# Two attention layers: scores of each head from its own 64 rows, rotation read from PSUM

## The chip, the core and the metric

The kernel runs on one core of a Trainium2 chip. What counts is the time of one execution on the device, in microseconds (us). TensorE (PE in the profile) multiplies matrices and writes its results to PSUM, which has eight banks per partition; VectorE (DVE), ScalarE (ACT) and GpSimd (POOL) work between PSUM and SBUF; SyncE (SP) starts transfers. Each engine goes through its own list of instructions in order and waits at semaphores for the others.

## What is computed

The program holds two blocks of a model on one sequence of 256 tokens, with 16 meta tokens in front (T = 272 columns). The first block has four layers: attention (layer 0), an mLSTM, an HGRN2, attention again (layer 3). The change is in the two attention layers, which compute this:

```
q, k, v, z = split(u @ w_in)                   # 16 query heads, 4 key heads, 64 features each
q = rope(rmsnorm(q, q_gain), pos)              # per head; rope: x1*cos - x2*sin, x2*cos + x1*sin
k = rope(rmsnorm(k, k_gain), pos)              # x1, x2 = first and second 32 features
s = q . k / 8                                  # a block of 128 queries: its own 128 keys and those before
s = where(0 <= dist < 128 and valid, s, -inf)
m = max(max(s), sink)
p = exp(s - m) / (sum(exp(s - m)) + exp(sink - m))
y = (p @ v) * silu(z) @ w_out
```

## The kernel before

**Layout.** Features lie on partitions and tokens on columns. A tile of 128 features holds two heads. The layer works in two halves `hf`, each with one key tile, four query tiles `n` and one value tile: 2 key heads and 8 query heads. Before, the columns of the weights were permuted (`turned`), so that a tile's 128 rows are: first 32 features of head 0, first 32 of head 1, second 32 of head 0, second 32 of head 1. So the rotation swaps the upper and the lower 64 rows, but the rows of one head are not together. To separate the two heads, `key` writes two copies of K (`kp`), each with the other head's rows set to zero.

**Projections.** A projection tile is 24 matmuls (8 groups of weight rows, each as three passes L402, L403, L404 of split high and low parts); half a tile, 12 matmuls, is the `unit` in which the order of TensorE is counted. The split weights `whi` and `wlo` come by two ways: a DMA by SP with a cast L389 on ScalarE and a subtraction L395 on VectorE, or DMAs by POOL (L329, L337) with a pass L336 on ScalarE between them.

**Key and query.** `key` and `query` take a finished projection from PSUM: Square for the norm (L695, L742), a copy with the gain (L697, L745), two copies of 64 rows for the swapped halves (`swap`, L594), then on VectorE a product with cos, a product with sin and a sum (L699 to L701, L751 to L753). A matmul over the squares gives the sums for the norm (L705, L759).

**Scores.** One step of `scores` (L831 to L856) takes one query block `bq` (1 or 2) and one tile n: a matmul L838 of 128 rows against both masked K copies, 2 x 144 or 2 x 256 columns in one bank, and a matmul L839 that adds the mask; then the maximum (L843, VectorE), small operations (L844 to L846), one exp for the sink (L847), one exp per head with its sum (L850, ScalarE), and the division (L852 to L855). `turn` (L863 to L868) transposes p on TensorE, `values` (L878, L880) multiplies by v, `gate` (L922) and a split (L585, L586) make the input `MH`, `ML` of the output projection, which runs in two parts of 96 matmuls, the second one for the features of the second half. Layer 0 has also a first block of 16 queries, done by `short`.

**Order.** TensorE's order is written by hand: `Flow` keeps a list of due times in units, and after each half tile it puts in what is due. Steps follow each other `D_ST` units apart (A0_ST = 1.5, A3_ST = 1), eight in a half; `turn` comes `D_PT` units after its step. The other engines' orders are made by a scheduler. PSUM banks by name (`PB`): mm 3, s 2, t 1, g 1, a 1; scores take from s, projections from mm.

## Time and profile before

| | before |
|---|---|
| three runs | 1418.65, 1420.56, 1421.35 us |
| median | 1420.56 us |
| profiled execution | 1422.77 us |
| its span (first to last instruction) | 1421.0 us |
| mean granted TensorE clock | 0.993 |
| TensorE busy | 1356.4 us, 95% |
| VectorE / ScalarE / POOL busy | 992.2 / 804.6 / 446.6 us |

Start times in all rows count from the start of the span. Layer 0 lies between some 15 and 128 us, layer 3 between some 637 and 742 us. "Busy" is the sum of an engine's instructions; matmuls overlap in their pipeline, so the distance from one start to the next tells more than a matmul's own duration. In brackets stands the idle time of an engine before an instruction and who ended it.

### The profile page before, as it was taken

To read this page: it belongs to the slowest core of one execution; us is meant where nothing else is said; L and a number is where in the kernel's file an instruction comes from. 1 tells how busy PE (TensorE), PEld (TensorE's weight loads), DVE (VectorE), ACT (ScalarE), POOL (GpSimd) and SP (SyncE) were. 2 spreads that over 40 slices of the span, in tenths; PEclk is the share of its full clock that TensorE was granted. 3 is DMA by queue.
4 is the path that set the end of the run, shared out by engine and by line. 5 is a ranking of instruction groups with operands and counts; after the bars stand their busy time and mean duration, and the time that the engine had idled before them with its cause. 6 is when DMAs were issued, how large, how long until landed. Compare 5 with 4: busy or idle time off the path is not lost.

```text
span 1421.0 us, 27398 instructions
## 1 busy us (share of the span) xinstructions
PE 1356.4 (95%) x10347; PEld 1261.1 (89%) x10347; DVE 992.2 (70%) x2424; ACT 804.6 (57%) x1700; POOL 446.6 (31%) x611
## 2 busy tenths in 40 slices
PE   6999999999899999998999999999999899999997
PEld 5878989999899888898778888999999789899986
DVE  5865569999776767687656676787645576687744
ACT  6875655556644454448675586454444667455532
POOL 3322468778703434123224511300014340400000
PEclk9999999999999999999999999999999999999999
DMA  9989999999568988559889973456564994466662
GB/s 275 283 186 209 230 242 247 231 238 242 135 185 234 253 180 196 134 179 247 191 171 237 259 193 104 144 189 195 180 198 151 265 239 125 119 193 194 186 184 89
DMA packets 79349, 281.88 MB, mean 198 GB/s; under 512 B 9024, under 2 KB 10184, under 8 KB 79216
## 3 DMA queue, kind: packets, MB, share of 16 engines
q0 software_dynamic: 44512, 160.74, 49.0%
q1 hardware_dynamic: 34272, 118.60, 26.0%
q8 instruction: 81, 1.33, 0.4%
q10 hardware_dynamic: 432, 0.79, 0.1%
q14 instruction: 52, 0.43, 0.1%
HBM read 279.01 MB, written 1.07 MB: 197 GB/s over the span
## 4 chain that ended last, share of the span: by engine, by line
PE 72%; DVE 10%; DMA 6%; ACT 5%; issue 4%; POOL 2%; SPq 0%; DVEq 0%; POOLq 0%; ACTq 0%
PE pmm L402 14%; PE pmm L403 14%; PE pmm L404 14%; DMA wraw<-in_wts_dram 2%; PE ps L404 2%; PE ps L403 2%; PE ps L402 2%; DVE wlo L395 2%; DMA wlo<-in_wts_dram 2%; PE ps L838 1%; DMA whi<-in_wts_dram 1%; PE pa L878 1%; PE ps L1270 1%; PE pt L863 1%; PE pmm L1893 1%
## 5 line engine op out<-in xcount | busy, mean ns | idle before, releaser
L402 PE MATMUL pmm<-XH,whi 128*128 128x272 f32 (+1 forms) x1544 | 458.1, 298 | 17.5 <-ACT whi L389 10.8
L404 PE MATMUL pmm<-XH,wlo 128*128 128x272 f32 (+1 forms) x1544 | 444.8, 289 | 8.5 <-DMA wlo<-in_wts_dram 7.9
L403 PE MATMUL pmm<-XL,whi 128*128 128x272 f32 (+1 forms) x1544 | 445.4, 289 | 2.6 <-DVE XL L533 2.6
L389 ACT CAST whi<-wraw 128x1024 fp32r<-128x1024 f32 (+1 forms) x211 | 217.8, 1033 | 242.5 <-DMA wraw<-in_wts_dram 180.4
L395 DVE TENSOR_TENSOR wlo<-wraw,whi 128x1024 fp32r<-128x1024 f32 (+1 forms) x211 | 256.5, 1217 | 96.5 <-PE pmm L404 43.3
L402 PEld LDWEIGHTS pmm<-XH,whi 128*128 128x128 f32 x1544 | 294.4, 191 | 31.7 <-ACT whi L389 10.8
L404 PEld LDWEIGHTS pmm<-XH,wlo 128*128 128x128 f32 x1544 | 294.9, 191 | 10.0 <-DMA wlo<-in_wts_dram 8.5
L403 PEld LDWEIGHTS pmm<-XL,whi 128*128 128x128 f32 x1544 | 295.0, 191 | 4.4 <-DVE XL L533 3.7
L336 ACT ACTIVATE wlo<-whi 128x1024 fp32r<-128x1024 f32 (+1 forms) x150 | 157.9, 1054 | 86.4 <-PE pmm L404 39.8
L337 POOL DMA_DIRECT2D wlo<-in_wts_dram x150 | 130.5, 873 | 212.3 <-ACT wlo L336 101.1
L402 PE MATMUL pmm<-MH,whi 128*128 128x256 f32 (+1 forms) x624 | 182.3, 292 | 0.6 <-DVE HT L966 0.6
L329 POOL DMA_DIRECT2D whi<-in_wts_dram x150 | 89.5, 598 | 296.7 <-PE pmm L404 235.9
L403 PE MATMUL pmm<-ML,whi 128*128 128x256 f32 (+1 forms) x624 | 177.9, 285 | 1.5 <-DVE ML L586 0.8
L404 PE MATMUL pmm<-MH,wlo 128*128 128x256 f32 (+1 forms) x624 | 177.3, 284 | 0.0
L402 PEld LDWEIGHTS pmm<-MH,whi 128*128 128x128 f32 x624 | 117.7, 189 | 7.8 <-issue 6.2
L403 PEld LDWEIGHTS pmm<-ML,whi 128*128 128x128 f32 x624 | 117.9, 189 | 2.2 <-DVE ML L586 1.1
L404 PEld LDWEIGHTS pmm<-MH,wlo 128*128 128x128 f32 x624 | 118.1, 189 | 0.0
L404 PE MATMUL ps<-XH,wlo 128*128 128x256 f32 (+1 forms) x256 | 72.5, 284 | 1.4 <-DVE wlo L395 1.4
L403 PE MATMUL ps<-XL,whi 128*128 128x256 f32 (+1 forms) x256 | 72.9, 285 | 0.0
L402 PE MATMUL ps<-XH,whi 128*128 128x256 f32 (+1 forms) x256 | 72.0, 283 | 0.0
L404 PEld LDWEIGHTS ps<-XH,wlo 128*128 128x128 f32 x256 | 48.7, 190 | 1.6 <-DVE wlo L395 1.6
L403 PEld LDWEIGHTS ps<-XL,whi 128*128 128x128 f32 x256 | 48.4, 189 | 0.0
(933 smaller groups left out, 2870.2 us busy)
## 6 DMA issues: line engine op xcount, KB each, us to landing
wraw<-in_wts_dram SPq DMA_DIRECT2D x209, 512.0 KB, 4.4
whi<-in_wts_dram POOLq DMA_DIRECT2D x148, 512.0 KB, 6.4
wlo<-in_wts_dram POOLq DMA_DIRECT2D x148, 512.0 KB, 7.8
wraw<-in_wts_dram SPq DMA_DIRECT2D x16, 384.0 KB, 3.5
nb<-drb POOLq DMA_DIRECT2D x8, 272.0 KB, 6.4
HT<-in_xt_dram SPq DMA_DIRECT2D x4, 272.0 KB, 9.7
nb<-drf POOLq DMA_DIRECT2D x8, 128.0 KB, 4.9
whi<-in_wts_dram POOLq DMA_DIRECT2D x2, 384.0 KB, 6.9
```

The lines of the kernel that those rows point to most:

```text
L329: nc.gpsimd.dma_start(hi[:, :c1 - c0], src)
L336: act(lo[:, :w], hi[:, :w].bitcast(F32), AF.Copy, scale=-1.0)
L337: nc.gpsimd.dma_start(lo[:, :w], src, accum_op=ALU.add)
L389: nc.scalar.copy(hi[:, :c1 - c0], raw[:, :c1 - c0])
L395: V.tensor_tensor(lo[:, :c1 - c0], raw[:, :c1 - c0], hi[:, :c1 - c0].bitcast(F32), op=ALU.subtract)
L402: PE.matmul(ps, c.hi(b), xh, start=first, stop=False)
L403: PE.matmul(ps, c.hi(b), xl, start=False, stop=False)
L404: PE.matmul(ps, c.lo(b), xh, start=False, stop=last)
L838: PE.matmul(sv, qp[:, n, qs], kp[:, :, k0:k1], start=True, stop=False)
L863: PE.transpose(pt[:c1 - c0, (2 * y + x) * P:(2 * y + x + 1) * P], p_[:, x, c0:c1], K["ident"])
L878: PE.matmul(po[64 * x:64 * x + 64, :], vt[:kk, bq - 1 + y, 64 * x:64 * x + 64], pT[:kk, y, x].rearrange("p n t -> p (n t)"), start=y == 0, ...
L1270: PE.matmul(sl[:, 0:P], s["kw"], halves_of(kq, CB_[0], T + CA[0], b), start=True, stop=True)
```

## The change

- The weights' columns are no longer permuted: a head's 64 features lie together, head 0 in rows 0 to 63 and head 1 in rows 64 to 127.
- `scores(n)` now does both query blocks of a tile n at once. Each head has a bank of its own: four matmuls with 64 rows each (two blocks, two heads), then one mask matmul of 400 columns per bank. So a step takes both s banks; a half has four steps, A0_ST = 3 and A3_ST = 2.5 units apart. The exps of the sinks go in one instruction of four columns.
- The masked copies of K are gone; only for `short` in layer 0 two copies of 16 columns (`k0`) remain.
- `rotate` reads the projection from PSUM: four copies of 32 rows on ScalarE, a product from PSUM on VectorE, a product, a sum. The gains are in four tables (`kc`, `ks`, `qc`, `qs`), made once in each of the two layers on POOL from cos and sin and two columns of gains.
- p_ has four buffers instead of three.

The core of the diff:

```diff
-A0_KN, A0_VT, A0_QN, A0_RS, A0_AT, A0_ST, A0_PT, A0_VA, A0_S0, A0_START = 2, 2, 2, 5, 1, 1.5, 4.5, 1, 6.5, 8
-A3_KN, A3_VT, A3_QN, A3_RS, A3_AT, A3_ST, A3_PT, A3_VA, A3_S0, A3_START = 1.5, 2, 3, 5.5, 2.5, 1, 4, 1, 6, 10.5
+A0_KN, A0_VT, A0_QN, A0_RS, A0_AT, A0_ST, A0_PT, A0_VA, A0_S0, A0_START = 2, 2, 2, 5, 1, 3, 4.5, 1, 6.5, 8
+A3_KN, A3_VT, A3_QN, A3_RS, A3_AT, A3_ST, A3_PT, A3_VA, A3_S0, A3_START = 1.5, 2, 3, 5.5, 2.5, 2.5, 4, 1, 6, 10.5
...
-    head = p // 32 % 2
+    head = p // 64
     put("blk", (head[:, None] == head[None]).astype(np.float32))
-    put("selH", (head[:, None] == np.arange(2)[None]).astype(np.float32))
+    put("selA", (head[:, None] == np.arange(2)[None]).astype(np.float32))
+    put("selH", ((p // 32 % 2)[:, None] == np.arange(2)[None]).astype(np.float32))
...
-    sg = np.where(p < 64, -1.0, 1.0).astype(np.float32)[:, None]
+    sg = np.where(p % 64 < 32, -1.0, 1.0).astype(np.float32)[:, None]
...
+        if "A2" in names:
+            K["A12"] = t.bitcast(BF)[:, CB.at["A1"] - o:CB.at["A2"] - o + CB.size["A2"]]
...
+    HEADS = ((0, 32, 32), (32, 0, 32)) + LATENT
...
+            def table(n):
+
+                if n not in tables:
+                    first_consts()
+                    tables[n] = [wk.tile([P, T], F32, name=n + x, bufs=1) for x in "cs"]
+                    for t, x, g in zip(tables[n], ("cosA", "sinA"), (f"a{n}g", f"a{n}s")):
+                        G.tensor_scalar(t, K[x], smc(g, j), None, op0=ALU.mult)
+                return tables[n]
+
+            tables = {}
+
+            def rotate(ps, n, c0, dst):
+
+                c, si = (t[:, c0:] for t in table(n))
+                sw = wk.tile([P, T], F32, name="sw", bufs=SWB)[:, c0:]
+                for d, s_, m in HEADS:
+                    nc.scalar.copy(sw[d:d + m], ps[s_:s_ + m])
+                V.tensor_mul(dst, ps, c)
+                V.tensor_mul(sw, sw, si)
+                V.tensor_add(dst, dst, sw)
...
-                    act(kg, psk, AF.Copy, scale=smc("akg", j))
-                    ks = swap(wk, kg, HALVES)
-                    V.tensor_mul(kg, kg, K["cosA"])
-                    V.tensor_mul(ks, ks, K["sinA"])
-                    V.tensor_add(kg, kg, ks)
+                    rotate(psk, "k", 0, kg)
...
-                        V.tensor_mul(kg, kg, rk)
-                        kp = wk.tile([P, 2, T], F32, name="kp")
-                        for x in range(2):
-                            act(kp[:, x], kg, AF.Copy, scale=K["selH"][:, x:x + 1])
-                        D["kp"] = kp
+                        D["kp"] = wk.tile([P, T], F32, name="kp")
+                        V.tensor_mul(D["kp"], kg, rk)
+                        if not last:
+                            D["k0"] = wk.tile([P, 2, NM], F32, name="k0")
+                            for x in range(2):
+                                act(D["k0"][:, x], D["kp"][:, :NM], AF.Copy, scale=K["selA"][:, x:x + 1])
...
-                    qg = wk.tile([P, T], F32, name="qg", bufs=3)
-                    act(qg[:, q0:], psq, AF.Copy, scale=smc("aqg", j))
                     if n == 0:
                         D["qp"] = wk.tile([P, 4, T], F32, name="qp")
-                    qp = D["qp"]
-
-                    qs = swap(wk, qg, HALVES, q0)
-                    V.tensor_mul(qp[:, n, q0:], qg[:, q0:], K["cosA"][:, q0:])
-                    V.tensor_mul(qs[:, q0:], qs[:, q0:], K["sinA"][:, q0:])
-                    V.tensor_add(qp[:, n, q0:], qp[:, n, q0:], qs[:, q0:])
+                    rotate(psq, "q", q0, D["qp"][:, n, q0:])
...
-                        PE.matmul(ps0[:NM, 32 * n:32 * n + 32], qp[:, n, 0:NM], kp[:, :, 0:NM], start=True, stop=True)
+                        PE.matmul(ps0[:NM, 32 * n:32 * n + 32], qp[:, n, 0:NM], D["k0"], start=True, stop=True)
...
-                def scores(bq, n, pT):
-                    qs = slice(*BLOCKS[bq])
-                    k0, k1 = (0, 144) if bq == 1 else (16, 272)
-                    nk = k1 - k0
-                    mk = K["A1"] if bq == 1 else K["A2"]
-                    ps = mx("s")
-                    sv = ps[:, :2 * nk].rearrange("p (h k) -> p h k", h=2)
-                    PE.matmul(sv, qp[:, n, qs], kp[:, :, k0:k1], start=True, stop=False)
-                    PE.matmul(sv, K["identb"], mk[:, None, :].to_broadcast([P, 2, nk]), start=False, stop=True)
-                    st = wk.tile([P, 8], F32, name="sta", bufs=3)
-                    nm, es, dn, rd = (st[:, 2 * x:2 * x + 2] for x in range(4))
-                    rr, n2 = rqT[:, bq, 2 * n:2 * n + 2], nk8[:, 2 * n:2 * n + 2]
-                    V.tensor_reduce(nm, sv, axis=AX, op=ALU.max, negate=True)
-                    V.tensor_mul(nm, nm, rr)
-                    V.tensor_tensor(nm, nm, n2, op=ALU.min)
-                    V.tensor_sub(es, nm, n2)
-                    act(es, es, AF.Exp)
-                    p_ = wk.tile([P, 2, 256], F32, name="p_", bufs=3)
+                def scores(n, pTs):
+
+
+                    ps = [mx("s"), mx("s")]
+                    seg, ks = (slice(0, 144), slice(144, 400)), (slice(0, 144), slice(16, 272))
+                    for b in range(2):
+                        for x in range(2):
+                            xs = slice(64 * x, 64 * x + 64)
+                            PE.matmul(ps[x][:, seg[b]], qp[xs, n, slice(*BLOCKS[b + 1])], kp[xs, ks[b]], start=b == 0,
+                                      stop=False)
                     for x in range(2):
-                        act(p_[:, x, :nk], sv[:, x, :], AF.Exp, bias=nm[:, x:x + 1], scale=rr[:, x:x + 1],
-                            accum_out=dn[:, x:x + 1])
-                    V.tensor_add(dn, dn, es)
-                    V.reciprocal(rd, dn)
-                    for x in range(2):
-                        V.tensor_scalar(p_[:, x, :nk], p_[:, x, :nk], rd[:, x:x + 1], None, op0=ALU.mult)
-                    fl.later(D_PT, lambda: turn(bq, n, p_, pT))
+                        PE.matmul(ps[x][:, :400], K["identb"], K["A12"], start=False, stop=True)
+                    st = wk.tile([P, 16], F32, name="sta", bufs=3)
+                    nm, es, dn, rd = (st[:, 4 * x:4 * x + 4] for x in range(4))
+                    by = lambda t: t.rearrange("p (b x) -> p b x", b=2)
+                    rr = rqT[:, 1:3, 2 * n:2 * n + 2]
+                    n2 = nk8[:, None, 2 * n:2 * n + 2].to_broadcast([P, 2, 2])
+                    for b in range(2):
+                        for x in range(2):
+                            V.tensor_reduce(nm[:, 2 * b + x:2 * b + x + 1], ps[x][:, seg[b]], axis=AX, op=ALU.max,
+                                            negate=True)
+                    V.tensor_tensor(by(nm), by(nm), rr, op=ALU.mult)
+                    V.tensor_tensor(by(nm), by(nm), n2, op=ALU.min)
+                    V.tensor_tensor(by(es), by(nm), n2, op=ALU.subtract)
+                    p_ = [wk.tile([P, 2, 256], F32, name="p_", bufs=4) for _ in range(2)]
+                    for b in range(2):
+                        nk, y = (144, 256)[b], slice(2 * b, 2 * b + 2)
+                        for x in range(2):
+                            z = slice(2 * b + x, 2 * b + x + 1)
+                            act(p_[b][:, x, :nk], ps[x][:, seg[b]], AF.Exp, bias=nm[:, z],
+                                scale=rr[:, b, x:x + 1], accum_out=dn[:, z])
+                        if b == 0:
+                            act(es, es, AF.Exp)
+                        V.tensor_add(dn[:, y], dn[:, y], es[:, y])
+                        V.reciprocal(rd[:, y], dn[:, y])
+                        for x in range(2):
+                            V.tensor_scalar(p_[b][:, x, :nk], p_[b][:, x, :nk], rd[:, 2 * b + x:2 * b + x + 1], None,
+                                            op0=ALU.mult)
+                        fl.later(D_PT + b, lambda b=b: turn(b + 1, n, p_[b], pTs[b]))
...
-                def step(bq, n, pT):
-                    if n == 0:
-                        pT = wk.tile([P, 2, 2, 4, P], F32, name="pT")
-                    scores(bq, n, pT)
-                    if bq == 1 or n < 3:
-                        fl.later(D_ST, lambda: step(bq if n < 3 else 2, (n + 1) % 4, pT))
+                def step(n, pTs):
+                    scores(n, pTs)
+                    if n < 3:
+                        fl.later(D_ST, lambda: step(n + 1, pTs))
                     elif hf == 0:
                         busy["att"] = False
                         for f in busy["wait"]:
                             fl.later(D_ST, f)
 
+                def first_step():
+                    step(0, [wk.tile([P, 2, 2, 4, P], F32, name="pT") for _ in range(2)])
+
                 def begin():
                     busy["att"] = True
                     if last:
-                        step(1, 0, None)
+                        first_step()
                     else:
                         short()
-                        fl.later(D_ST, lambda: step(1, 0, None))
+                        fl.later(D_ST / 2, first_step)
...
-        acol += [1024 + turned(r(128 * hf, 128 * hf + 128)), turned(qcols[512 * hf:512 * hf + 512]),
+        acol += [1024 + r(128 * hf, 128 * hf + 128), qcols[512 * hf:512 * hf + 512],
...
-    put("aqg", np.concatenate([f["a_q_gain"]] * 2, 1)[:, turned(r(0, 128))].T)
-    put("akg", np.concatenate([f["a_k_gain"]] * 2, 1)[:, turned(r(0, 128))].T)
+    for n in "qk":
+        g = np.concatenate([f[f"a_{n}_gain"]] * 2, 1)
+        put(f"a{n}g", g.T)
+        put(f"a{n}s", g[:, r(128) ^ 32].T)
```

**TensorE, first scores of layer 0.** `pmm` are projections, `ps` the s banks, `kp` and `qp` keys and queries, `ca` holds the mask and its identity. Before:

```order
238 L404 MATMUL pmm<-XH,wlo 128x272
239 L838 MATMUL ps<-kp,qp 128x288
240 L839 LDWEIGHTS ca
241 L839 MATMUL ps<-ca 128x288
242 L402 MATMUL pmm<-XH,whi 128x272
...
253 L404 MATMUL pmm<-XH,wlo 128x272
254 L838 MATMUL ps<-kp,qp 128x288
255 L839 LDWEIGHTS ca
256 L839 MATMUL ps<-ca 128x288
```

After, at the same place:

```order
238 L406 MATMUL pmm<-XH,wlo 128x272
239 L853 MATMUL ps<-kp,qp 128x144 x2
240 L853 MATMUL ps<-kp,qp 128x256 x2
241 L856 LDWEIGHTS ca
242 L856 MATMUL ps<-ca 128x400
243 L856 LDWEIGHTS ca
244 L856 MATMUL ps<-ca 128x400
245 L404 MATMUL pmm<-XH,whi 128x272
...
280 L406 MATMUL pmm<-XH,wlo 128x272
281 L853 MATMUL ps<-kp,qp 128x144 x2
282 L853 MATMUL ps<-kp,qp 128x256 x2
```

The second group of scores stood 12 projections behind the first and took the other bank; it now stands 36 behind and takes both banks again.

**ScalarE, layer 3, ahead of the first exps.** `sqq` is the Square of a query tile, `sw` the swapped rows, `wlo` the weight cast. Before:

```order
699 L742 ACTIVATE sqq<-pmm 128x256
700 L745 ACTIVATE qg<-pmm,sm 128x256
701 L336 ACTIVATE wlo<-whi 128x1024
702 L714 ACTIVATE kp<-kg,ce 128x272 x2
703 L594 COPY sw<-qg 64x256 x2
704 L850 ACTIVATE p__8812,sta<-ps,sta,rqT 128x144 x2
705 L847 ACTIVATE sta<-sta 128x2
706 L850 ACTIVATE p__8841,sta<-ps,sta,rqT 128x144 x2
```

After:

```order
672 L763 ACTIVATE sqq<-pmm 128x256
673 L680 COPY sw<-pmm 32x256 x4
674 L338 ACTIVATE wlo<-whi 128x1024
675 L763 ACTIVATE sqq<-pmm 128x256
676 L680 COPY sw<-pmm 32x256 x4
677 L338 ACTIVATE wlo<-whi 128x1024
678 L874 ACTIVATE p__8830,sta<-ps,sta,rqT 128x144 x2
679 L874 ACTIVATE p__8831,sta<-ps,sta,rqT 128x256
680 L877 ACTIVATE sta<-sta 128x4
681 L874 ACTIVATE p__8831,sta<-ps,sta,rqT 128x256
```

The two masked K copies are gone, and the exps of the second block stand directly behind those of the first.

**POOL, start of layer 3.** `nsa` are sums for the norm of the layer's input, `whi` and `wlo` the weight transfers. Before:

```order
376 L329 DMA whi<-in_wts_dram 128x1024
377 L491 TENSOR_TENSOR nsa<-nsq 128x272
378 L491 TENSOR_TENSOR nsa<-nsq,nsa 128x272 x5
379 L329 DMA whi<-in_wts_dram 128x1024 x4
380 L337 DMA wlo<-in_wts_dram 128x1024 x4
```

After:

```order
379 L331 DMA whi<-in_wts_dram 128x1024
380 L670 TENSOR_SCALAR kc<-ce,sm 128x272
381 L670 TENSOR_SCALAR ks<-ce,sm 128x272
382 L670 TENSOR_SCALAR qc<-ce,sm 128x272
383 L670 TENSOR_SCALAR qs<-ce,sm 128x272
384 L493 TENSOR_TENSOR nsa<-nsq 128x272
385 L493 TENSOR_TENSOR nsa<-nsq,nsa 128x272 x5
386 L331 DMA whi<-in_wts_dram 128x1024 x4
```

The four tables stand ahead of the norm sums; in layer 0 they stand ahead of the last norm sum. There, the norm matmuls of TensorE (L495, L496) have moved from its row 23 to its row 73.

## Rows read from the trace of the kernel before

**Rows 1.** The page: busy time of each engine; then the chain that ended last.
```profile
PE 1356.4 (95%) x10347; PEld 1261.1 (89%) x10347; DVE 992.2 (70%) x2424; ACT 804.6 (57%) x1700; POOL 446.6 (31%) x611
...
PE 72%; DVE 10%; DMA 6%; ACT 5%; issue 4%; POOL 2%; SPq 0%; DVEq 0%; POOLq 0%; ACTq 0%
```

**Rows 2.** Busy time by stretches of layers 0 and 3; the first row names the columns.
```profile
core 0: us, PE busy (x) PEld busy (x) DVE busy (x) ACT busy (x) POOL busy (x), PEclk, DMA share, GB/s
35.00:70.00 35.00, 35.00 (x276) 31.04 (x276) 29.91 (x106) 28.11 (x79) 10.64 (x15) 1.00 1.08 284
...
665.00:690.00 25.00, 21.20 (x136) 16.43 (x135) 19.65 (x80) 20.01 (x62) 6.72 (x10) 0.93 1.02 248
690.00:712.00 22.00, 19.78 (x136) 15.03 (x134) 12.41 (x51) 15.18 (x46) 4.83 (x7) 1.00 0.80 167
```

**Rows 3.** TensorE's waits from 637 to 742: releaser, us in total, times, longest.
```profile
PE ps L838 <- ACT p__8812 L850: 3.8, 1, 3.8
PE ps L838 <- ACT p__9297 L850: 1.9, 1, 1.9
```

**Rows 4.** TensorE in order of time, two score steps: start, us, engine, line, operation.
```profile
52.37 0.65 PE L838 MATMUL ps<-kp,qp 128*128 128x288 f32 x2
52.86 0.29 PE L839 MATMUL ps<-ca 128*128 128x288 bf16 x1
...
53.11 0.29 PE L403 MATMUL pmm<-XL,whi 128*128 128x272 f32 x1
...
680.37 1.02 PE L838 MATMUL ps<-kp,qp 128*128 128x512 f32 x2
681.23 0.38 PE L839 MATMUL ps<-ca 128*128 128x512 bf16 x1
...
681.56 0.28 PE L403 MATMUL pmm<-XL,whi 128*128 128x256 f32 x1
```

**Rows 5.** TensorE in order of time, values matmul L878 with two heads.
```profile
77.48 2.08 PE L878 MATMUL pa<-pT,vt 16*64 16x512 f32 x8
79.49 0.66 PE L863 MATMUL pt<-ce,p__868 128*128 128x128 f32 x4
```

**Rows 6.** ScalarE in order of time, layer 3, ahead of the first exps.
```profile
668.72 0.39 ACT L742 ACTIVATE sqq<-pmm 128x256 f32<-128x256 f32 x1
669.00 0.47 ACT L745 ACTIVATE qg<-pmm,sm 128x256 f32<-128x256 f32 x1
669.36 1.06 ACT L336 ACTIVATE wlo<-whi 128x1024 fp32r<-128x1024 f32 x1
670.31 0.93 ACT L714 ACTIVATE kp<-kg,ce 128x272 f32<-128x272 f32 x2
671.25 0.82 ACT L594 COPY sw<-qg 64x256 f32<-64x256 f32 x2
672.09 0.47 ACT L850 ACTIVATE p__8812<-ps,sta,rqT 128x144 f32<-128x144 f32 x1
```

**Rows 7.** ScalarE in order of time, layer 0, the first exp.
```profile
56.43 0.45 ACT L850 ACTIVATE p__645<-ps,sta,rqT 128x144 f32<-128x144 f32 x1
```

**Rows 8.** Groups by shape: the larger reduce; count, busy us, mean ns.
```profile
L843 DVE TENSOR_REDUCE sta<-ps 128x2 f32<-128x512 f32 x16 | 11.1, 692 | 11.7 <-PE ps L839 11.6
```

**Rows 9.** Groups by shape: a table-like product on POOL; count, busy us, mean ns.
```profile
L1435 POOL TENSOR_SCALAR nf<-pr 128x256 f32<-128x256 f32 x12 | 15.8, 1320 | 0.4
```

**Rows 10.** POOL in order of time, layer 3, after its norm sums.
```profile
641.12 2.18 POOL L329 DMA_DIRECT2D whi<-in_wts_dram  x4 [4.27 <-DVE rt L448]
```

**Rows 11.** TensorE in order of time, start of layer 0: norm sums.
```profile
20.23 1.11 PE L495 MATMUL pa<-nsa,ones 128*128 128x272 f32 x2
...
22.27 0.43 PE L404 MATMUL pmm<-XH,wlo 128*128 128x272 f32 x1
```

**Rows 12.** ScalarE and VectorE after the last values matmul of layer 3.
```profile
735.93 0.59 ACT L880 COPY Y<-pa 128x512 f32<-128x512 f32 x1 [0.82 <-PE pa L878]
...
738.23 1.42 DVE L586 SCALAR_TENSOR_TENSOR ML<-zs,MH 128x256 fp32r<-128x256 f32 x4
```

More of the change, by code (lines that the diff above doesn't have):

```diff
@@ L123 @@
 SM = Cols()
-for _n, _c in (("ng", 32), ("gpm", 16), ("gqm", 16), ("gpf", 16), ("gqf", 16), ("aqg", 2), ("akg", 2),
+for _n, _c in (("ng", 32), ("gpm", 16), ("gqm", 16), ("gpf", 16), ("gqf", 16), ("aqg", 2), ("akg", 2), ("aqs", 2), ("aks", 2),
                ("sink", 32), ("convw", 64), ("convb", 16), ("gb", 1), ("hg", 16), ("gam", 32), ("og", 8),
@@ L129 @@
 CS = Cols()
-for _n, _c in (("ident", 128), ("blk", 128), ("selH", 2), ("E", 32), ("cosA", T), ("sinA", T), ("sel0", 16),
+for _n, _c in (("ident", 128), ("blk", 128), ("selH", 2), ("selA", 2), ("E", 32), ("cosA", T), ("sinA", T), ("sel0", 16),
                ("inv", 1), ("sgnH", 2), ("sgnM", 1), ("selM", 1), ("selN", 1),
@@ L293, in load_masks @@
             K[x] = t.bitcast(BF)[:, CB.at[x] - o:CB.at[x] - o + CB.size[x]]
+        if "A2" in names:
+            K["A12"] = t.bitcast(BF)[:, CB.at["A1"] - o:CB.at["A2"] - o + CB.size["A2"]]
     def first_consts():
         if "ident" not in K:
-            load_consts(("ident", "blk", "selH", "E", "cosA", "sinA", "sel0", "inv", "sgnH", "sgnM", "selM", "selN"),
+            load_consts(("ident", "blk", "selH", "selA", "E", "cosA", "sinA", "sel0", "inv", "sgnH", "sgnM", "selM", "selN"),
                         "ce")
```

## The prediction

> **What bounds the kernel now.** I read the page first, then the busy table of the two attention layers by stretches, then TensorE's waits there, then single stretches in order of time. TensorE is busy 95% of the span and holds 72% of the chain that ended last [rows 1]. In layer 0 it never waits in the stretches that hold the first half's scores: 35.00 of 35 us are busy, at full clock [rows 2]. There only fewer or shorter TensorE instructions help, and a new wait costs its full length. Layer 3 is different: 665 to 690 has 21.20 busy of 25 us and a mean granted clock of 0.93, and 690 to 712 has 19.78 of 22 [rows 2]. Two waits of the score matmul L838 explain most of it, 3.8 us and 1.9 us, both for exps (L850) that still read its bank [rows 3]. So I look for two things: TensorE time per score step, and who frees the two banks "s" how late.
>
> **Scores on TensorE.** Now a step is one head pair and one query block: two L838 matmul passes and one mask matmul. A step of 288 columns starts at 52.37; the second projection after it starts at 53.11 and the first about 0.125 earlier, so the step's slot is 0.61 us. A step of 512 columns runs from 680.37 to 681.56 less 0.12: 1.07 us [rows 4]. Both together, one n of four: 1.69 us. There are 4 n, 2 halves, 2 layers: 16 of them, 27.0 us.
> After the change one n is four matmuls with 64 rows (144 and 256 columns, two heads) and two masks of 400 columns. The two passes of 512 columns take 0.86 us, from 680.37 to the mask's start at 681.23 [rows 4], so 144 and 256 columns cost 0.24 and 0.43. A mask pass takes the rest of the slot, 0.21 for 512 columns, 0.17 for 400. If the two heads run beside each other in the two row halves of the array, both blocks take 0.67 us; if one after the other, 1.34. The masks take 2 x 0.17. No matmul pair on row halves stands in this trace. The nearest row is L878, which puts two heads side by side in the column halves: its eight passes of 512 columns would be 3.41 us in a row and 1.71 side by side, and the next instruction starts 2.01 us after the first [rows 5]. So halves do run beside each other, and entering and leaving this form costs up to 0.30 for two such groups. I take 0.67 + 0.33 + 0.30 = 1.30 us; the bounds are 1.20 and 1.45. Gain: 16 x 0.39 = **+6.2 us** (3.8 to 7.8), all on the path, since in layer 0 TensorE is the bound and in layer 3 projections follow directly.
> The Trainium skill, "TensorE: Matmul & The Clock Gate", Part 3, states that tiles in different row groups run at the same time, and gives 3.07 times for four row tiles. No run here shows row tiles; L878 agrees for column tiles, 2.01 against 3.41 us. Taken as an estimate of 3.07 parts in 4 for our pair, the 0.67 would be 0.87, one n 1.50, the gain 3.0 us and the whole sum +1.5 us, which the partial-overlap rival below covers.
>
> **The two banks.** Today a step takes one of two "s" banks, so a step may be issued while the one before it is still read. After the change each step fills both, and the next n must wait until all four reduces and four exps of this n are done. The chain behind one n: four reduces, about 1.3 us together (the 512-column reduce of today takes 0.69 [rows 8]), three small operations 0.45, four exps with their accumulator reads: two of 144 elements at 0.46 each [rows 6], two of 256 at an estimated 0.56 (0.46 and 112 elements more), and the small exp, 2.2: some 4 us, plus whatever stands ahead in the queues of VectorE and ScalarE. The steps are 3 and 2.5 units apart, 36 or 24 to 36 projections with transposes between them.
> - Layer 0, first half, second n: its scores come 36 projections (4.5 us) after those of the first n. In ScalarE's order the next query tile (Square and four copies) and a weight cast L336 (1 us) still stand ahead of the first exps, which start at 56.43 today [rows 7]; there the second bank hides it. With 1.2 us more exps of the second block behind them, the banks come free near 59.7 and TensorE is there at 57.8: **-2.0 us** (0 to -3).
> - Layer 0, other n: two groups of 12 projections more plus transposes lie between, 5.4 to 6.6 us against about 4 and queueing: nothing taken.
> - Layer 3, second n (today's 3.8 us): from 668.72 to the first exp at 672.09 ScalarE does a Square, a gain copy (0.36), a cast (0.95), the two masked K copies (0.94) and two swap copies (0.84) [rows 6]. The masked copies go and the other copies become four of 32 rows, about the same in sum (below), so the exps begin 0.9 us sooner, at 671.2; but four of them and the small one, 2.2 us, must end before both banks are free: near 673.4, against some 673.1 today. The norm matmul of a query tile now lies ahead of that step, so TensorE arrives later and has more behind it: a stall of 3.3 instead of 3.8, **+0.5 us** (-1 to +5). The half clock behind it I keep.
> - Layer 3, the 1.9 us stall near 711: it is the third of four quick steps of the second half, 12 projections apart; that crowd is gone: **+1.9 us**. In its place six later steps, 24 projections and two transposes apart (about 4.6 us) against a 4 to 5 us chain: 0.3 us each, **-2.0 us** (0 to -4).
>
> **Rotation, tables, masks.** VectorE keeps three operations per tile; that one of them reads PSUM is its only change. ScalarE drops a gain copy (0.36) and two copies of 64 rows (0.82), 1.18 us per tile, for four copies of 32 rows from PSUM. Such a copy does not stand in the trace; the Square from PSUM, 0.28 to the next start, and a 64-row copy, 0.41, bound it: 1.1 to 1.6 us for four, and I take 1.2, nearer the row that reads PSUM. Per half the two K mask copies go, 0.93 [rows 6]. All this lies beside TensorE and is worth nothing by itself; where ScalarE is waited for, it is counted above. A projection's bank is now held until VectorE's product has read it; the two other mm banks cover that for two tiles of 24 projections, 3 us each. I take nothing, and a VectorE later than that would be a new wait, worth what it exceeds 3 us. The four table products per layer go to POOL. No such product stands in the trace; the nearest is a tensor-scalar on 128x256, 1.32 us [rows 9], so up to 5.3 us for four. In layer 3 POOL idles 4.27 us before its four weight DMAs at 641.12 because TensorE has not yet freed the buffers [rows 10]; the tables fit in, and 0 to 1 us of these DMAs is late. In layer 0 they stand ahead of the last norm sum. That moves the norm matmuls L495/L496 on TensorE fifty rows down, two projection tiles later. Today they run from 20.23 to about 22.04 (22.27 less one projection of 0.23) [rows 11], 1.81 us; the projections around them are 0.23 apart, against 0.125 at 52 us, so this is the lower of the clock's two levels (1.2 GHz). Later, at 2.4 GHz, they cost 0.9: +0.9. The first values that need the norm are wanted only some 10 us later, but a split on VectorE now waits ahead of the fourth tile: -0.5. Together **+0.4 us** (-2 to +0.9).
> The last values matmul of layer 3 now has 24 projections (2.9 us) of the first output part behind it, before 48. The chain from its copy at 735.93 to the first low half at 738.6 takes 2.7 us [rows 12]: just covered. With POOL I set **-0.3 us** (0 to -1.5).
>
> **How the numbers follow.** 6.2 - 2.0 + 0.5 + 1.9 - 2.0 + 0.4 - 0.3 = +4.7 us. The profiled execution took 1422.77 us, so it would take 1418.1; the median of the runs before is 1420.56, 2.2 less, and gives **1416 us**, 0.33% faster. A measurement here tells 0.2% (2.8 us) from no change, so faster means under 1417.7, slower over 1423.4.
>
> **Rivals.**
> - *The banks become the bound.* All 14 steps that follow another in their layer wait longer than the sum has it. At 0.35 us more for each the gain is gone (1421), at 0.7 us it is 1426. For it: ScalarE is busy 20.01 and VectorE 19.65 of 25 us in 665 to 690 [rows 2], so a microsecond of queueing is easy. Against it: 690 to 712 is calmer, ScalarE 15.18 of 22 [rows 2], and in layer 0 there are 1.5 to 2 us to spare. Chance 0.25, of which 0.14 ends within 0.2% and 0.11 slower. The Trainium skill, "TensorEngine Tiling (Array Packing)", PSUM Bottleneck, warns of just this: tiling speeds up TensorE and not the emptying of PSUM. The two waits of [rows 3] agree with it.
> - *The two heads don't run beside each other.* This one ends slower by a single mechanism. Its place is the four matmuls of each n, its price 0.67 us more per n, so 2.0 us against 1.69 now: -5.0 instead of +6.2, the sum -6.5, 1427 us. It decides from 1.59 us per n on, where the sum is zero. Against it: L878 [rows 5]. For it: no pair on row halves was measured here. Chance 0.09.
> - *They overlap in part.* At half overlap the streams take 1.0 us, one n 1.63, the sum -0.6, 1421 us. Chance 0.08, within 0.2%.
> - *Layer 3's first stall goes as well*, with the half clock after it (0.93 over 25 us [rows 2] is 1.7 us lost): 3.3 + 1.7 us more, 1411 us. It needs ScalarE to be free before 670; the cast and the two tiles' copies ahead of the exps [rows 6] speak against it. Chance 0.14.
> - *The forecast as it stands:* 0.44, of which 0.08 falls within 0.2%, where the scores cost near 1.45.
>
> Faster 0.36 + 0.14 = 0.50, the same 0.08 + 0.14 + 0.08 = 0.30, slower 0.11 + 0.09 = 0.20. The range from 1409 to 1426 takes in the bounds of the scores term and of the stalls, the partial overlap and most of the bank case; it leaves out the serial case and the far ends, together under 0.2. The forecast's own range is 1412 to 1419.
>
> **What would show it.** In the profile after: per n, from the first 64-row matmul to the projection that follows, 1.2 to 1.45 us, with the two heads' matmuls starting within 0.05 us of each other (serial: 0.24 apart or more, 2.0 us). Among TensorE's waits, one of about 2 us for an exp near 58 us in layer 0, one of about 3 us in layer 3 and small ones behind it, none near 711. Mean granted clock still near 0.93 in that stretch. The norm matmuls near 29 us at full clock. The forecast is wrong if waits for exps sum to over 10 us in both layers, or if layer 0 shows none.

## The result

The changed kernel takes 1437.62 us (median of 4 runs, 1434.67 to 1440.08) where the kernel before took 1420.12 on the same chip: a ratio of 1.0118, 95% interval 1.0093 to 1.0143. It is 17.5 us slower. The forecast was 1416 us, in a range from 1409 to 1426. The profiled execution took 1435.70 us, its span is 1433.9. The two profiled executions differ by 12.9 us, less than the medians do; the account below explains those 12.9.

The projections are the same 8172 matmuls in both kernels, so the start of the same projection shows where the time goes. All times count from the start of the span:

| the same projection | before | after | difference |
|---|---|---|---|
| layer 0, ahead of the first scores | 47.26 | 50.06 | +2.8 |
| end of layer 0 | 133.28 | 146.84 | +13.6 |
| ahead of layer 3 | 632.30 | 646.93 | +14.6 |
| behind layer 3 | 766.74 | 782.14 | +15.4 |
| the last one | 1351.39 | 1364.07 | +12.7 |

Nearly all is lost in layer 0, where TensorE had no wait from 35 to 128 us before. Layer 3, which had the waits, comes out level. First the page of the changed kernel, the rows that answer to [rows 1]:

```profile
PE 1355.4 (95%) x10411; PEld 1263.0 (88%) x10411; DVE 988.8 (69%) x2408; ACT 805.2 (56%) x1700; POOL 455.2 (32%) x619
...
PE 66%; DVE 12%; ACT 9%; issue 6%; DMA 4%; POOL 3%; SPq 0%; DVEq 0%; POOLq 0%; ACTq 0%
```

TensorE's part of the chain fell from 72% to 66%; ScalarE's rose from 5% to 9%. The engines do no more work than before: somebody waits. Busy time by stretches of the changed kernel, columns as in [rows 2]:

```profile
35.00:70.00 35.00, 30.61 (x246) 26.84 (x244) 27.47 (x91) 26.31 (x71) 9.46 (x14) 1.00 1.01 242
70.00:100.00 30.00, 24.13 (x183) 21.03 (x184) 16.36 (x77) 17.73 (x59) 6.49 (x9) 0.94 0.78 171
100.00:128.00 28.00, 25.69 (x180) 19.55 (x179) 15.04 (x60) 15.35 (x45) 5.74 (x9) 0.94 0.61 129
665.00:690.00 25.00, 21.65 (x165) 19.46 (x165) 19.43 (x58) 19.57 (x47) 8.67 (x13) 0.93 1.06 247
```

The first of these had 35.00 of 35 us busy before. Two stretches of layer 0 now have a granted clock of 0.94 as well. The largest of TensorE's waits in layer 0, 35 to 145 us, of the changed kernel (total, times, longest):

```profile
PE pt L890 <- ACT pT L895: 3.5, 3, 2.1
PE pt L890 <- ACT pT L835: 3.2, 2, 1.8
PE ps L853 <- ACT p__666 L874: 1.7, 1, 1.7
PE pt L787 <- DVE rk L451: 1.5, 1, 1.5
PE ps L808 <- ACT p__991 L874: 1.5, 1, 1.5
PE pt L833 <- ACT pT L895: 0.6, 1, 0.6
```

L890 is the transposition of p, L833 that of the first 16 queries, L895 and L835 the copies that empty their bank "t" on ScalarE. Their three rows are 7.3 us, more than all waits for the s banks (L853, L808: 3.2). The longest of them, TensorE in order of time:

```profile
92.49 0.29 PE L406 MATMUL pmm<-XH,wlo 128*128 128x272 f32 x1
92.71 0.95 PE L853 MATMUL ps<-kp,qp 64*128 64x144 f32 x8
93.59 0.51 PE L856 MATMUL ps<-ca 128*128 128x400 bf16 x2
93.80 0.43 PE L404 MATMUL pmm<-XH,whi 128*128 128x272 f32 x1
94.07 0.28 PE L405 MATMUL pmm<-XL,whi 128*128 128x272 f32 x1
...
95.45 0.60 PE L890 MATMUL pt<-ce,p__990 128*16 128x128 f32 x4
...
99.67 0.66 PE L890 MATMUL pt<-ce,p__991 128*128 128x128 f32 x4 [2.10 <-ACT pT L895]
```

And ScalarE in the same microseconds:

```profile
95.65 1.06 ACT L338 ACTIVATE wlo<-whi 128x1024 fp32r<-128x1024 f32 x1 [2.58 <-PE pmm L406]
96.62 0.45 ACT L874 ACTIVATE p__1118<-ps,sta,rqT 128x144 f32<-128x144 f32 x1
...
98.05 0.56 ACT L874 ACTIVATE p__1119<-ps,sta,rqT 128x256 f32<-128x256 f32 x1
...
99.01 0.34 ACT L894 COPY pT<-pt 16x256 f32<-16x256 f32 x1
99.26 0.36 ACT L895 COPY pT<-pt 128x256 f32<-128x256 f32 x1
```

The transposes of the first block (p__990) fill bank t from 95.45 to 96.05. ScalarE is at a weight cast then, and in its list the four exps of the next n (p__1118, p__1119) come before the copies, which start at 99.01. The transposes of the second block (p__991), a unit behind the first, need the same bank and wait 2.10 us.

The row behind L835 (3.2 us) has a part of its own. Between the two transposes of a first n stands that of the first 16 queries (L833), a third user of bank t. At 71.27 the second block waits 1.77 us for its copy L835, which stood behind the exps and a weight cast of 1.06 us; at 113.22 it waits 1.39 us for it behind a weight cast and a pass on z, with no exp in between. So ScalarE's list holds the bank each time, but not always by the exps.

### The profile page after: what moved, and what is told of

Its sections match the earlier page's. It is cut to its first block, busy times and chain, and to the rows that moved or that the text cites. A ratio compares the mean times of both kernels' runs of the same rounds, so it can differ in the third digit from the quotient of the medians.

```text
span 1433.9 us, 27500 instructions
## 1 busy us (share of the span) xinstructions
PE 1355.4 (95%) x10411; PEld 1263.0 (88%) x10411; DVE 988.8 (69%) x2408; ACT 805.2 (56%) x1700; POOL 455.2 (32%) x619
## 3 DMA queue, kind: packets, MB, share of 16 engines
q8 instruction: 82, 1.34, 0.4%
## 4 chain that ended last, share of the span: by engine, by line
PE 66%; DVE 12%; ACT 9%; issue 6%; DMA 4%; POOL 3%; SPq 0%; DVEq 0%; POOLq 0%; ACTq 0%
PE pmm L404 13%; PE pmm L405 13%; PE pmm L406 13%; PE ps L406 2%; DVE wlo L397 2%; PE ps L405 2%; PE ps L404 2%; ACT wlo L338 2%; DMA wlo<-in_wts_dram 1%; ACT sw L680 1%; PE ps L1298 1%; DMA whi<-in_wts_dram 1%; PE pmm L1921 1%; PE pmm L1923 1%; PE pmm L1922 1%
## 5 line engine op out<-in xcount | busy, mean ns | idle before, releaser
L404 PEld LDWEIGHTS ps<-XH,whi 128*128 128x128 f32 x256 | 48.6, 190 | 0.0
```

Of the source, the lines that this page charges most:

```text
L404: PE.matmul(ps, c.hi(b), xh, start=first, stop=False)
```

## The theories

**Turns (T):** the loss lies in bank t. A score step now makes two sets of p at a time, so two sets of transposes follow each other 12 projections apart, and ScalarE's list puts the next n's four exps ahead of the copies that empty the one bank. **Rotation (R):** the loss comes from the rotation that reads PSUM and from the tables. The runs were made against both. Ratios are to the kernel before on the same chip. Beside each stand the differences of the same projections from the kernel before, in one profiled execution each, counted from its first projection. The first of these columns is called the lag below. The kernel before with one edit that removes no wait of layer 0 (e6) differs by 1 to 2 us in such a column, so less than that says nothing.

| run | median us | ratio (95%) | ahead of first scores | end of layer 0 | layer 3 alone |
|---|---|---|---|---|---|
| changed kernel | 1437.6 | 1.0118 (1.0093 to 1.0143) | +2.5 | +13.3 | +0.8 |
| e1 two t banks | 1423.9 | 1.0024 (1.0004 to 1.0044) | +1.9 | +5.0 | -5.1 |
| e2 transposes later | 1429.2 | 1.0069 (1.0044 to 1.0093) | +2.3 | +9.5 | -0.1 |
| e3 rotation from SBUF | 1433.0 | 1.0085 (1.0062 to 1.0109) | -0.5 | +8.0 | +1.2 |
| e4 rotation alone | 1422.5 | 1.0018 (1.0003 to 1.0034) | +1.9 | +3.5 | -1.4 |
| e5 e1 and e3 | 1423.2 | 1.0010 (0.9994 to 1.0027) | +0.6 | +1.7 | -1.6 |
| e6 before, two t banks | 1418.2 | 0.9991 (0.9970 to 1.0012) | -1.1 | -1.1 | -1.8 |
| e7 e5, spaced | 1433.9 | 1.0097 (1.0074 to 1.0119) | +0.8 | +8.9 | +4.1 |
| e8 copies on VectorE | 1428.8 | 1.0067 (1.0042 to 1.0093) | +3.2 | +8.2 | -1.1 |
| e9 rotation by layer | 1420.6 | 1.0003 (0.9985 to 1.0021) | +0.6 | +2.4 | -2.2 |
| e10 e9, first queries in bank a | 1418.1 | 0.9975 (0.9959 to 0.9992) | +0.9 | +0.7 | -3.8 |
| e11 e1, layer 0's tables on VectorE | 1422.0 | 1.0013 (0.9991 to 1.0036) | +1.3 | +2.8 | -3.4 |

## Bank t

**e1: a second bank for the transposes.** In these two layers bank g holds only the norm sums otherwise.

```diff
-                    pt = mx("t")
+                    pt = mx("t" if bq == 1 else "g")
```

> The changed kernel, but the transposes of the second block's p go into bank g instead of t. Theory T (turns): the loss sits in the transposes of p (L890), which wait for the one t bank because ScalarE copies it out behind the next n's exps; the waits of L890 in layer 0 (2.10, 1.02 and 0.35 us behind L895) and most of layer 3's 4.7 us go, with the half clock after them: 5 to 9 us less than the changed kernel, about 1430 us. Theory R (rotation): the loss comes from the rotation read from PSUM (1.95 us of ScalarE per tile against 1.51, and VectorE's product behind it) and the tables on POOL; two t banks change nothing, 1436 to 1439 us.

1423.88 us: 13.7 us less than the changed kernel, more than T had put on it. TensorE's waits of e1 in layer 0, same stretch:

```profile
PE ps L853 <- ACT p__666 L874: 1.7, 1, 1.7
PE pt L787 <- DVE rk L451: 1.5, 1, 1.5
PE pa L905 <- ACT pT L894: 1.4, 1, 1.4
PE ps L808 <- ACT p__991 L874: 1.1, 1, 1.1
PE pt L833 <- ACT pT L895: 0.6, 1, 0.6
```

By the ratios, each against its own chip's kernel before, it is 13.3 us. All rows of L890 are gone. Part of the delay returns as the values matmul's wait for the late copies (L905, 1.4). The granted clock is 1.00 again in the two stretches that had 0.94, but the stretch ahead of them, 1.00 in the changed kernel, now has 0.95; e1 in the three:

```profile
35.00:70.00 35.00, 31.11 (x234) 27.42 (x232) 26.23 (x87) 25.14 (x68) 8.81 (x12) 0.95 1.01 239
70.00:100.00 30.00, 27.48 (x223) 22.53 (x221) 18.08 (x82) 19.84 (x65) 7.57 (x11) 1.00 0.87 187
100.00:128.00 28.00, 27.42 (x214) 22.70 (x212) 17.51 (x69) 19.51 (x60) 8.14 (x13) 1.00 0.76 171
```

The lower clock cost the changed kernel up to 3.5 us in layer 0 (0.06 of 58 us); e1 still loses 1.8 (0.05 of 35), with no L890 wait left. So the waits for bank t cost their own length, and of that clock about half can be theirs. By the table, 8.3 us (13.3 less 5.0) come back in layer 0 and 5.9 in layer 3.

**e2: the same by time.** The transposes come 1.5 units later, where the exps ahead of their copies have run. The edit, shortened to the values that change:

```diff
-A0_PT = 4.5, A3_PT = 4
+A0_PT = 6, A3_PT = 5.5
```

> The changed kernel with A0_PT 6 instead of 4.5 and A3_PT 5.5 instead of 4: the transposes of p come 1.5 units later, at the time of the scores after next, when the exps ahead of their copies have run. Theory T: 5 to 10 us less than the changed kernel, 1428 to 1433 us. Theory R: no change, 1436 to 1439 us.

1429.20 us, 8.4 less than the changed kernel, as T said. The L890 rows of layer 0 fall from 6.7 to 1.6 us (1.3 behind L895, 0.3 behind L835), but the end of the layer now waits for its values (MH, 1.6):

```profile
PE pmm L404 <- ACT MH L587: 1.6, 1, 1.6
...
PE pt L890 <- ACT pT L895: 1.3, 2, 0.6
```

**e8: the same bank, another copier.**

```diff
-                    nc.scalar.copy(pT[:m, 0, :, n, :], ptv[:m, 0])
-                    nc.scalar.copy(pT[:, 1, :, n, :], ptv[:, 1])
+                    V.tensor_copy(pT[:m, 0, :, n, :], ptv[:m, 0])
+                    V.tensor_copy(pT[:, 1, :, n, :], ptv[:, 1])
```

> The changed kernel with one t bank, but the copies of the transposed p (L894, L895) on VectorE instead of ScalarE. Theory T says it is ScalarE's queue (the next n's exps ahead of the copies) that holds the bank: the L890 waits fall below half, 1426 to 1432 us. If one bank is too few for any copier, or VectorE's own queue (divisions of p that wait for the same exps) holds it as long: 1435 us or more.

1428.83 us, 8.8 less (7 by the ratios). The L890 waits of layer 0 fall from 6.7 to 3.5 us, just not below half; in layer 3 they go altogether. Of the waits for t in layer 0, those behind L895 have gone, with VectorE as copier; those behind L835, which ScalarE still copies, remain:

```profile
PE pt L890 <- ACT pT L835: 3.5, 2, 2.4
PE ps L853 <- ACT p__666 L874: 1.7, 1, 1.7
```

With VectorE as copier one t bank is enough for the transposes that wait behind L895. It is ScalarE's list that holds the bank there, not the single bank by itself.

**e6: the kernel before with two t banks,** the edit of e1 made there.

> Control: the kernel before with the second block's p transposes in bank g. Theory T: the waits for the t bank are a product of the new order, the kernel before has none of them, so no change, 1418 to 1423 us. If the t bank was a hidden cost all along: 1415 us or less.

1418.16 us, ratio 0.9991 with 1.0 inside its interval. In layer 0 the kernel before has no wait for bank t to lose. In layer 3 it has one, 1.1 us of L863 behind a copy of the norm factors (rqT, L777), which goes here; a gain is not clear of the noise. The waits of L890 are made by the new order.

## Rotation and tables

**e4: the new rotation alone,** in the kernel before, with its features and its scores.

```diff
-                    act(kg, psk, AF.Copy, scale=smc("akg", j))
-                    ks = swap(wk, kg, HALVES)
...
+                    rotate(psk, "k", 0, kg)
```

> The kernel before (its scores, its masked K copies, its order of features) with the new rotation alone: four copies of 32 rows from PSUM, product from PSUM, tables on POOL. Theory T: within 3 us of before, 1418 to 1423 us. Theory R: most of the loss is here, 1428 to 1436 us.

1422.47 us, ratio 1.0018: about 2 to 2.5 us slower, as T said. Most of it is at the start of layer 0, where e4 has the waits that the changed kernel has, the longest of them (35 to 60 us):

```profile
PE pt L785 <- DVE rk L449: 1.5, 1, 1.5
```

Later in the layer it waits once more for bank t, 1.4 us at the transposition of the first 16 queries (L831), with the old scores: the rotation alone makes one such wait.

**e3: the new scores with the rotation from SBUF,** no tables. Core of the edit:

```diff
+                act(gg, ps, AF.Copy, scale=smc(f"a{n}g", j))
...
                 for d, s_, m in HEADS:
-                    nc.scalar.copy(sw[d:d + m], ps[s_:s_ + m])
-                V.tensor_mul(dst, ps, c)
+                    nc.scalar.copy(sw[d:d + m], gg[s_:s_ + m])
+                V.tensor_mul(dst, gg, K["cosA"][:, c0:])
...
```

> The changed kernel with the rotation as before in kind: ScalarE copies the projection with its gain to SBUF, the four copies of 32 rows read that copy, VectorE multiplies by the plain cos and sin; no tables on POOL. One instruction of 0.37 us per tile more on ScalarE, but VectorE's first product need not wait for the four copies. Theory T: within 3 us of the changed kernel, or slower by ScalarE's 0.37 us per tile, 1436 to 1441 us. Theory R by the tables or by VectorE's wait: 6 to 12 us less, 1426 to 1432 us. Theory R by ScalarE's length alone: slower, 1440 us or more.

1432.97 us, 4.7 less than the changed kernel, between the two theories. The lag ahead of the first scores goes from +2.5 to -0.5, with L787's wait, although ScalarE has one instruction more per tile. Layer 3 gains nothing: it has one wait of 5.4 us for the first exps there instead.

What in the rotation lags, two rows of the changed kernel tell, ScalarE's and VectorE's:

```profile
54.32 1.54 ACT L680 COPY sw<-pmm 32x272 f32<-32x272 f32 x4
```

```profile
55.89 0.44 DVE L681 TENSOR_TENSOR qp<-pmm,qc 128x272 f32<-128x272 f32 x1 [1.22 <-ACT sw L680]
```

The product from PSUM doesn't use the copies, yet starts only when the fourth has ended. Both read the same bank there. In e3, where both read the same tile in SBUF, the product starts beside the copies (at 27.65, with the copies from 27.59 to 29.29). And the four copies take 1.54 us, not 1.2.

**e11: layer 0's tables on VectorE,** otherwise e1.

```diff
-                        G.tensor_scalar(t, K[x], smc(g, j), None, op0=ALU.mult)
+                        (G if last else V).tensor_scalar(t, K[x], smc(g, j), None, op0=ALU.mult)
```

> As the run with two t banks alone, but layer 0's four tables are made on VectorE, not POOL; POOL's norm sums and weight DMAs are back in their old order. If the tables on POOL cause the lag of 2.2 us at the start of layer 0 (at 47 us): the lag falls below 1 us and the time by 1 to 2.5 us, 1421 to 1423 us. If the lag comes from the rotation itself (VectorE's PSUM product starts only when ScalarE's four copies end): the lag stays at 2 us or more, 1424 us or above.

1421.99 us. L787's wait falls from 1.5 to 0.3 while a new one of 0.6 for ScalarE's Square (L773) comes in; the lag goes from 1.9 to 1.3 us, which is between the two expectations and a change that one profiled execution can't tell from none. The time lies in the first one's range, but its interval overlaps e1's. So how much the tables and how much VectorE's wait make of the lag is left open.

## Both mends, and a kernel that beats both

**e5: e1 and e3 together.**

> Both mends at once: the second block's p transposes into bank g, and the rotation from an SBUF copy with plain cos and sin, no tables. Theory T with R as the smaller part: the two add up, since the one lies in the score steps and the other at the start of layer 0: 1423.9 less 2.5 to 4.6, so 1419 to 1421.5 us, level with the kernel before or slightly better. If ScalarE is the next limit (2.4 us per query tile instead of 1.95): no better than two t banks alone, 1424 us or more.

1423.15 us, outside the range expected, with a ratio of 1.0010, since the kernel before takes 1421.96 on this chip: level with it, but barely better than e1. Layer 0 nearly adds up, +1.7 at its end, where the gains of e1 and e3 together (8.3 and 5.3) give -0.3; layer 3 doesn't, since the SBUF rotation brings back a wait of 4.9 us for the first exps.

**e7: e5 with more room** for the second n of each half and the values. The edit, shortened:

```diff
-                        fl.later(D_ST, lambda: step(n + 1, pTs))
+                        fl.later(D_ST + (n == 0), lambda: step(n + 1, pTs))
-A0_VA = 1, A3_ST = 2.5, A3_PT = 4
+A0_VA = 2, A3_ST = 3, A3_PT = 4.5
```

> As the run with both mends, and the second n of each half a unit later (1.5 us), the values matmul of layer 0 a unit later, layer 3 with 3 units between steps and the transposes at 4.5: the remaining waits of L853 for the exps (1.2 us in layer 0, 1 to 5 in layer 3) and of L905 for pT (1.4 us) go. Theory T: 2 to 5 us less than both mends alone, 1414 to 1418 us. If the end of the layer becomes the bound: 1420 us or more.

1433.93 us: 11 us worse than e5 where 2 to 5 us less were expected. Its waits in layer 0:

```profile
PE ps L798 <- ACT p__1034 L864: 3.2, 1, 3.2
PE pt L880 <- DVE p__673 L871: 2.2, 1, 2.2
PE pmm L404 <- ACT MH L587: 1.6, 1, 1.6
```

The wait for the second n went (1.2), but the first queries of the next half (L798) came upon exps that had moved later, and the end of the layer waits for MH. Layer 3 has a new wait of 3.7 us for exps, too. A step moved away from one neighbour runs into the next.

**e9: each rotation where it suits,** with two t banks: from SBUF in layer 0, from PSUM with tables in layer 3. Core of the edit:

```diff
+                if not last:
+                    act(gg, ps, AF.Copy, scale=smc(f"a{n}g", j))
+                    ps, c, si = gg, K["cosA"][:, c0:], K["sinA"][:, c0:]
+                else:
+                    c, si = (t[:, c0:] for t in table(n))
```

> Two t banks for p, and the rotation by layer: from an SBUF copy in layer 0 (no tables there), from PSUM with the tables in layer 3. Counted against the kernel before at the same projection, layer 0 cost 0.0 us with the SBUF rotation and two t banks, layer 3 gained 5 us with the PSUM rotation and 1.6 with the other. Theory: the layers are independent, so the two add up, 3 to 6 us less than the kernel before. If layer 3's gain came from the late start of layer 0: level with before, within 2 us.

1420.60 us, ratio 1.0003: most of the lag went, but the two did not add up. At the end of layer 0 the table has +1.7 for e5 and +2.4 here where the expectation counted 0.0, and layer 3 gained 2.2 us where e1's profile had shown 5.1. Two things make up these 2.9 us. e9 has a wait there that e1 lacks, for the copy of the norm factors that empties bank t, while e1 alone waits 0.6 us at L905:

```profile
PE pt L895 <- ACT rqT L796: 1.8, 1, 1.8
```

And from 665 to 690 the granted clock is 0.93 in e9 and 1.00 in e1, 1.8 us. That part belongs to the execution and not to the rotation: e11, whose layer 3 is that of e1 with the same waits, has 0.93 there, too, and -3.4 instead of -5.1; e10, whose layer 3 is that of e9, has 1.00 and -3.8 instead of -2.2.

**e10: and the first 16 queries' scores in bank a.**

```diff
-                    ps0 = mx("s")
+                    ps0 = mx("a")
```

> As the run by layer, and the scores of the first 16 queries in bank a instead of s, so that they need not wait for the exps of the half before (1.1 to 1.5 us of wait on L808). Theory of the banks: that wait goes, 1 us less than the run by layer, 4 to 7 us less than before. Rival: the values matmul of the same half then waits for bank a, no gain or 1 us more.

1418.08 us, ratio 0.9975 (0.9959 to 0.9992): faster than both kernels, by 1 to 6 us against the kernel before, and the only one of the eleven runs whose interval lies below 1. The wait on L808 went as expected and bank a made no new one, but 4 to 7 us less than before were expected and the medians differ by 2.1. Of the 12.6 us of waits that the changed kernel has in this part of layer 0, these are left:

```profile
PE ps L858 <- ACT p__674 L879: 1.2, 1, 1.2
PE pt L838 <- ACT pT L900: 0.6, 1, 0.6
PE pmm L406 <- DVE ML L397: 0.5, 1, 0.5
```

## Why the prediction was wrong

- **Scores on TensorE: right.** The step's slot in the rows above runs from 92.71 to 93.94 (94.07 less 0.125), 1.23 us, and it starts 0.10 later behind 92.49 than a projection would: 1.33 against 1.30 forecast, where it was 1.69. Eight passes take 0.88 us up to the masks, in 12 of the 16 steps; one head after the other would be 1.34. In these 12 the second head's matmul starts 0.005 to 0.007 us behind the first head's. The two heads do run beside each other in row halves, so the rival without overlap falls, and the one with part overlap (1.63 us). The gain is 16 x 0.36 = 5.8 us, forecast 6.2. The Trainium skill, "TensorE: Matmul & The Clock Gate", Part 3, had said that such tiles run at the same time; the prediction's estimate from its ratio for four tiles, 1.50 us for one n, was too high for this pair.
- **The two banks: the step that failed.** It said that the next n must wait for reduces and exps, and for the other n of layer 0 "nothing taken". For the s banks this was nearly right in layer 0: 1.7 us at the second n against 2.0 forecast, and 1.5 for the first 16 queries of the second half, which it had left out. The row of waits misses a part of the first: the bank of the second head comes free one exp later, and that time passes inside the step, whose way to the masks takes 1.51 instead of 0.88 us:

```profile
62.93 1.58 PE L853 MATMUL ps<-kp,qp 64*128 64x144 f32 x8 [1.68 <-ACT p__666 L874]
64.44 0.51 PE L856 MATMUL ps<-ca 128*128 128x400 bf16 x2
```

But the prediction ended its chain at the exps. Two transposes per n follow, and in layer 0 those of the first 16 queries, through a bank of which there is only one, emptied by the engine whose exps had just been put in a row of four. That step was never costed: 7.3 us of waits in layer 0 and 4.7 in layer 3. Up to 3.5 us of lower clock come on top in layer 0, half of which e1 has, too. e1 gives 13.7 us back by that bank alone. Its own sign of being wrong, waits for exps of over 10 us, did not show (5.6 us), since it counted exps alone. "The banks become the bound" was the right kind of rival, with the wrong bank and a price of 5 to 10 us instead of 14.
- **Layer 3: two errors of opposite sign, and the sum missed.** The forecast had some 3 us gained there, 8 x 0.39 by the scores and 0.4 by the waits; the table shows 0.8 lost. The waits for the s banks came out smaller than forecast: 1.2 us at the second n, not 3.3, and one more of 1.2 at the fourth in place of six small ones, each with another half microsecond inside the step. The 1.9 us wait near 711 is gone, the clock of 0.93 stays, as forecast. The transposes took what that gave, five waits, and the rotation adds three (L787 below, L725 and L751 with 0.7 each). The largest of TensorE's waits of the changed kernel from 637 to 760:

```profile
PE pt L890 <- ACT pT L895: 4.7, 5, 1.5
PE pt L787 <- DVE rk L451: 1.8, 1, 1.8
PE ps L853 <- ACT p__8831 L874: 1.2, 1, 1.2
PE ps L853 <- ACT p__9011 L874: 1.2, 1, 1.2
```

- **Rotation and tables: wrong sign.** +0.4 was forecast, within -2 to +0.9; e4 measures about -2. The norm matmuls did move, to 27.84, and take 0.9 us there, as forecast; that they ran at the lower clock before was read from the distance of the projections alone, the profile gives a granted clock of 1.00 from 17 to 24 us, with records that begin at 25. But VectorE's product waits for ScalarE's copies of the same bank, which was not considered; the copies of 32 rows cost 0.38 us each, near the upper bound, and the tables 4.85 us in layer 0 (1.16, 1.78, 0.96 and 0.95), within theirs. One reading was wrong without harm: the idle 4.27 us of POOL in layer 3 end with VectorE's rt, as the row says [rows 10], and not with a buffer that TensorE frees. The weight DMAs behind them were not late: they start at 654.82, 13.7 us later than before, where the projections are 14.6 later.
- **The sum.** Forecast +4.7. At the end of layer 0 the account is 8 x 0.36 = 2.9 us gained by the scores, 2.5 lost ahead of them, 3.2 by the s banks (1.7 and 1.5), 7.3 by bank t and 3.5 by the clock: 13.6 us lost, measured 13.3 (counted from the first projection; two terms left out, 0.6 us inside the step at 62.93 and a wait of 0.8 us at 130 that the kernel before alone has, nearly cancel). Layer 3 spends its own scores' gain on its waits. The warning of the Trainium skill, "TensorEngine Tiling (Array Packing)", PSUM Bottleneck, holds here: 2.9 us gained on TensorE in layer 0 against 10.5 us of waits for PSUM banks to be emptied, 7.3 of them for a bank that the tiled matmuls don't write. The prediction had quoted it and applied it to one of the two banks that a step passes.

## What to carry to other kernels

When small steps are merged into larger ones, follow every bank that a step passes through to the engine that empties it, not only the bank that the step fills; here the bank that was single and emptied by an engine with an in-order list became a wait when two of its users came close together. Check in that engine's list what stands between the fill and the copy. Where TensorE had no wait at all, a gain of a third of a microsecond per step was worth less than waits of 0.4 to 2.1 us at five of the eight steps.

## What the runs showed of the hardware

Two fp32 matmuls of 64 rows in the upper and lower half of the array, each into its own bank, run beside each other: their starts lie 0.005 to 0.007 us apart, and eight passes of 144 and 256 columns take 0.88 us with entry into the masks, against an estimated 1.34 one after the other, from the passes of 512 columns before [rows 4].

Copies on ScalarE of 32 rows by 272 columns from PSUM take 0.38 us each. From SBUF such a copy takes 0.42 us, as long as one of 64 rows (0.42): the number of rows is not what it costs. Four copies in a row of e3:

```profile
27.59 1.70 ACT L670 COPY sw<-qg 32x272 f32<-32x272 f32 x4
```

The same waits came with different granted clocks: layer 3 of e1 and e11 has the same waits and 1.00 against 0.93 from 665 to 690. What a wait costs in clock can't be read from one execution.
